# Where the third w_out block and the last modulation stand in a macaron block with pooling and RWKV-7

## The chip, the cores and the metric

One core of a Trainium2 chip runs the whole program once. The metric is the device time of one execution in microseconds (us). TensorE (PE) multiplies matrices, VectorE (DVE) and ScalarE (ACT) work element by element, and SyncE (SP) issues nearly all loads from HBM in one queue. The engines run side by side, each through its own list of instructions in a fixed order; an instruction that waits for another engine or a load holds up all that stand behind it in its list.

## What is computed

One sequence of 256 tokens of width 2048 goes through three sublayers: a gated feed-forward network (FFN), a mixer, and a second FFN. Each sublayer is wrapped in two norms and in a modulation by shift, scale and gate, nine vectors of 2048 that come from one matrix product of the condition `c` with `w_ada` (2048 x 18432, float32).

```python
mod = (silu(c) @ w_ada + b_ada).reshape(B, 3, 3, 2048)      # sublayer, (shift, scale, gate)

def sandwich_sublayer(x, fn, gain_pre, gain_post, shift, scale, gate, weight):
    h = rms_norm(x, gain_pre) * (1 + scale) + shift
    y = rms_norm(fn(h), gain_post)
    return x + weight * (1 + gate) * y

def hybrid_mixer(h, ...):
    p = h @ w_in
    y_pool = multiscale_pool(p[..., :512], ...)
    y_rwkv = rwkv7_time_mix(p[..., 512:], ...)               # 24 heads of 64
    return concatenate([y_pool, y_rwkv], -1) @ w_out         # 2048 x 2048

x = sandwich_sublayer(x, ffn1, ..., mod[0], weight=0.5)
x = sandwich_sublayer(x, hybrid_mixer, ..., mod[1], weight=1.0)
x = sandwich_sublayer(x, ffn2, ..., mod[2], weight=0.5)
```

The FFN is `(silu(h @ w_gate) * (h @ w_up)) @ w_down` with an inner width of 5632. All weights are float32.

## The kernel before

**Matmuls.** Float32 products are made of three matmuls: both operands are split into a rounded part (`hi`) and a rest (`lo`), and hi x hi, lo x hi and hi x lo are summed in PSUM. Weights come in raw tiles of up to 1 MB (`load`, line 174), and `split` (line 180) makes `hi` with a cast on ScalarE (line 186) and `lo` with a subtraction on VectorE (line 187). The activations are held split as `hT` (16 feature tiles of 128, for 256 tokens). All matmuls go through `mul` (line 201), so that most of them have line 202 in the profile.

**Who sets the order.** The program is written in the order of the functions below, but the lists of the engines are made by a scheduler at build time: it goes through the program with estimated durations and gives each engine, whenever it is free, the instruction that is ready and stands first in the program. A later instruction can so move ahead if an earlier one isn't ready. A tile waits for a free slot of its pool. Within the mixer's heads the list of TensorE is fixed by hand (`ordered`), as written. `split` is put 300 instructions ahead in the mixer.

**Modulation.** `ada_begin` (line 222) cuts the nine vectors into columns and the columns into four positions along the 2048 rows. Pre-norm shift and scale of the second FFN, `(7, 6)`, are cut in five, one for each k-block of that FFN (of 2, 2, 4, 4 and 4 feature tiles, `FIRST_BLOCKS`); gates are cut in two. A part of a position of the 4-tile blocks is 512 KB of `w_ada`, in two loads of 256 KB for `(7, 6)` and one of 512 KB for a gate, and one operation on VectorE (line 258) that multiplies it by a value of silu(c) and adds it to an accumulator. Four parts are a position, 16 parts a piece; behind a piece of `(7, 6)`, 16 matmuls with a column of ones (`ada_mod`, line 312) sum over the partitions, and VectorE adds the bias. `ada_step` (line 260) emits one position: load, sum, load, sum and so on. `ada_run` (line 274) is a generator for the mixer that emits one load, and the sum of three loads ago, at each call; it uses `x` (put off to HBM for the while) as its slots and does the modulation up to the third k-block of `(7, 6)`.

**The mixer's end.** The heads are worked off in six groups of two feature tiles (`rwkv_a`, `rwkv_b`), in stages of 12 slots (`stage`, line 883), with matmuls of weights between them as filling (`pieces`). In the last two stages the filling is `last_weights` (line 924): the pooling columns of `w_in`, then the first two of the four 512-column blocks of `w_out` (`out_piece`, line 912, one feature tile for both token halves at a time, six matmuls). The features come in the order 4 to 11, 0 to 3, 12, 13, and at last 14 and 15, which are the last group's heads (`late(14, 15)`). Of the 48 pieces 42 are taken in the two stages. Behind `late(14, 15)` come the other six, then the post-norm operations of these two blocks (`post_rows`), then blocks 2 and 3 with `rows_block` (line 597). Block 2 emits one `ada_step` with each of its four loads: the fourth k-block of `(7, 6)`. Raw tiles of the mixer have two slots, split tiles four.

**The second FFN's begin.** `outer` (line 632) goes over the five k-blocks. For each it makes the block's `hT` (`next_block`, with lines 423 to 428) and goes through ten weight loads, with a `tick` after each. Two of the ten are accumulated in PSUM over all k-blocks; the other eight are spilled to SBUF, and for these the first two k-blocks are merged: in the first k-block they only tick, and load nothing. There are four raw slots of 1 MB and four `ada` slots of 512 KB. Ticks 1, 3, 5 and 7 of the third k-block each emit one `ada_step` (the fifth k-block of `(7, 6)`); the last gate, `(8,)`, takes one step at every twelfth load of the row-wise phase that follows, where the scheduler may move it ahead.

Of the kernel before, what the change touches and what calls it, by code (L numbers as in the profile page):

```python
# [17 lines left out]
P = 128  # L18
# [11 lines left out]
TICKS2 = (1, 3, 5, 7)  # L30
GROUPS = (20, 16, 8)
ADA_AHEAD = ((7, 6), 2)
ADA_FFN1, ADA_FFN2 = 2.8, 12
# [49 lines left out]
class Block:  # L83
# [176 lines left out]
    def ada_step(self, psum):  # L260
        if self.ada_pos == len(self.ada_tasks):
            return
        cols, k0 = self.ada_tasks[self.ada_pos]
        width = cols[0][2]
        per = 512 // width
        if k0 == 0:
            self.acc = self.tile(self.accs, [P, 2, width], tag="acc")
        for kk in range(k0, k0 + 4, per):
            self.ada_sum(self.ada_load(cols, kk, per), self.acc, kk, per)
        self.ada_pos += 1  # L270
        if k0 == KD - 4:
            self.ada_mod(cols, self.acc, self.ada_sums(cols, self.acc), self.tile(psum, [P, 512], tag="mm"))

    def ada_run(self, upto, places):

        todo = []
        for cols, k0 in self.ada_tasks[self.ada_pos:self.ada_end[upto]]:
            per = 512 // cols[0][2]
            todo += [(cols, kk, per) for kk in range(k0, k0 + 4, per)]
        ready = []  # L280
        for n in range(len(todo) + len(places) - 1):
            if len(ready) == len(places) - 1 or n >= len(todo):
                cols, kk, per, raw = ready.pop(0)
                if kk == 0:
                    self.acc = self.tile(self.raws, [P, 4 * T], tag="ada", bufs=self.ada_bufs)[:, :2 * cols[0][2]]
                    self.acc = self.acc.rearrange("p (j c) -> p j c", j=2)
                self.ada_sum(raw, self.acc, kk, per)
            if n < len(todo):
                ready.append((*todo[n], self.ada_load(*todo[n], places[n % len(places)])))
            yield False  # L290
            if n >= len(places) - 1 and kk + per == KD:
                sums = self.ada_sums(cols, self.acc)
                yield True
                self.ada_mod(cols, self.acc, sums, self.bank(self.mod_bank))
                yield False
        self.ada_pos = self.ada_end[upto]
# [374 lines left out]
    def ffn(self, wg, wu, wd, every, mm, actp, blocks, block, outer_tick, first, spill, spare, groups, post_begin, post_done, ahead):  # L671
# [140 lines left out]
    def mixer(self, ctx):  # L812
# [67 lines left out]
        ada = self.ada_run(ADA_AHEAD, [flat_x[:, i * 4 * T:(i + 1) * 4 * T] for i in range(4)])  # L880
# [30 lines left out]

        def out_piece(q, kc):
# [62 lines left out]
        for q in range(2):  # L975
            for tt in range(2):
                self.post_rows(q, tt, 0, 512, banks[q][tt])
        for q, tags in ((2, ("pb", "zb")), (3, ("sb", "y", "mm"))):
            banks = [row(t) for t in tags]

            def load(kc):
                raw = self.load(I["w_out"], 4 * kc, 4, q * 512, 512)
                if q == 2:
                    self.ada_step(self.mm)
                return raw

            def done(tt, c0, n, ps):
                self.post_rows(q, tt, c0, n, ps)

            place = lambda tags: lambda shape: [self.tile(self.w2p, shape, F32R, tag=t) for t in tags]  # L990
            more = [place(t) for t in (("r", "k"), ("v", "bv")) * 2]
            self.rows_block(load, KD, 1, lambda k: self.hT[:, k], banks, q == 3, done, more, self.mm)
# [402 lines left out]
    def run(self):  # L1395
        I = self.I
        self.constants()
        with ExitStack() as ph:
# [15 lines left out]
            self.ffn(I["ffn1_w_gate"], I["ffn1_w_up"], I["ffn1_w_down"], ADA_FFN1, mm, actp, FIRST_BLOCKS, block, tick,  # L1414
# [5 lines left out]
        with ExitStack() as ph:  # L1420
            mm, actp = self.ffn_pools(ph)

            def block(k0, n):
                self.ada_finish(((7, 6), [b[0] for b in FIRST_BLOCKS].index(k0)), mm)
                self.next_block(2, k0, n, mm)

            def tick(q, i):
                if q == 2 and i in TICKS2:
                    self.ada_step(mm)

            self.ffn(I["ffn2_w_gate"], I["ffn2_w_up"], I["ffn2_w_down"], ADA_FFN2, mm, actp, FIRST_BLOCKS,
                     block, tick, FF_OUTER, FF_SPILL, (FF_SPILL + FF_OUTER) // 2 - 8, GROUPS,
                     lambda *a: (self.ada_finish((8,), mm), self.post_begin(2, 0.5, False, mm, *a)),
# [28 lines left out]
```

## Time and profile before

| | |
|---|---|
| median of 3 runs | 2132.65 us (2131.58 to 2134.56) |
| the profiled execution | 2132.83 us |
| its span, first to last instruction | 2131.0 us |
| granted TensorE clock, mean | 0.987 |
| bytes read from HBM | 499.87 MB, 237 GB/s over the span |

A row of the windows view has a stretch of time, the busy time and number of instructions of each engine in it, the granted clock of TensorE (1.00 is full), the busy share of the 16 DMA engines, and GB/s. A row of the order of time has start, duration, engine, line, operation, the tile written and the tiles read, their shape, how often, and in brackets the idle time of the engine before it and who ended it. `PEld` is the loading of the stationary operand, which overlaps the matmuls.

These stages matter here (us from the span's start): the last group's heads until about 1281, the rest of `w_out` until 1359, five padding matmuls and the norms until 1366, and the second FFN's k-blocks from there until about 1612.

### The profile page before, as it was taken

Reading aid. Unit: us, or ns where it says so; the run is one execution under the profiler, and the core shown is the slowest. Engines: PE = TensorE matmul, PEld = TensorE weight load, DVE = VectorE, ACT = ScalarE, POOL = GpSimd, SP = SyncE. Lnnn points to the kernel's source line nnn. Section 1 sums busy time; section 2 is a strip of 40 time slices with the busy share of each in tenths; the row PEclk is TensorE's granted clock in tenths of the full one; section 3 lists DMA queues with packets and bytes.
Section 4 is the critical chain, followed back from the end, with each engine's and each line's share of the span. In section 5 each row is a group of like instructions: output and inputs, shape, how many; then the busy total and the mean of one; then the engine's idle time right before and its main releaser. Section 6 shows DMA issues by size and latency. Waiting matters only on the chain.

```text
span 2131.0 us, 38906 instructions
## 1 busy us (share of the span) xinstructions
PE 2051.9 (96%) x16083; PEld 1829.5 (86%) x16083; DVE 1591.6 (75%) x2204; ACT 1010.5 (47%) x1483; POOL 0.2 (0%) x4
## 2 busy tenths in 40 slices
PE   3999999999999999999999997899999999999998
PEld 3999988888888888898999875789998888888887
DVE  6788898788887876688788968667996555555556
ACT  3544543444434455665555544453454344443453
POOL 0000000000000000000000000000000000000000
PEclk8999999999999999999999999899999999999999
DMA  8989888898989746565555567497875556555563
GB/s 303 352 315 315 291 284 323 308 331 311 320 320 321 267 145 195 174 192 157 147 166 158 167 217 266 158 324 246 317 280 197 190 187 196 181 194 191 187 195 121
DMA packets 315759, 506.62 MB, mean 238 GB/s; under 512 B 13013, under 2 KB 173886, under 8 KB 315070
## 3 DMA queue, kind: packets, MB, share of 16 engines
q1 hardware_dynamic: 314092, 500.78, 69.9%
q10 hardware_dynamic: 1490, 3.36, 0.5%
q8 instruction: 126, 2.06, 0.4%
q14 instruction: 51, 0.42, 0.1%
HBM read 499.87 MB, written 4.22 MB: 237 GB/s over the span
## 4 chain that ended last, share of the span: by engine, by line
PE 81%; DVE 4%; DMA 4%; ACT 1%; issue 1%; SPq 0%; DVEq 0%; ACTq 0%
PE mm L202 47%; PE mm L213 16%; PE mm L214 8%; PE ga L202 2%; PE sb L202 2%; PE sa L202 2%; DMA ada<-in_w_ada_dram 2%; DVE lo L187 1%; PE zb L202 1%; PE pb L202 1%; DMA raw<-in_w_out_dram 1%; PE y L202 1%; DVE acc L258 1%; DMA raw<-in_w_in_dram 1%; ACT hi L186 1%
## 5 line engine op out<-in xcount | busy, mean ns | idle before, releaser
L186 ACT CAST hi<-raw 128x1024 fp32r<-128x1024 f32 (+2 forms) x766 | 695.0, 913 | 873.7 <-PE mm L202 562.3
L187 DVE TENSOR_TENSOR lo<-raw,hi 128x1024 fp32r<-128x1024 f32 (+2 forms) x766 | 799.2, 1051 | 398.8 <-ACT hi L186 396.3
L202 PE MATMUL mm<-hT,hi 128*128 128x256 f32 x3648 | 671.0, 286 | 11.9 <-DVE hT L428 7.2
L202 PEld LDWEIGHTS mm<-hT,hi 128*128 128x128 f32 x3648 | 565.1, 190 | 27.5 <-DVE hT L428 9.0
L213 PE MATMUL mm<-hT,hi 128*128 128x512 f32 x1536 | 539.9, 395 | 0.0
L202 PE MATMUL mm<-hT,lo 128*128 128x256 f32 x1824 | 511.3, 281 | 0.8 <-DVE lo L187 0.7
L214 PE MATMUL mm<-hT,lo 128*128 128x256 f32 x1536 | 431.7, 281 | 0.1
L202 PE MATMUL mm<-hi,act 128*128 128x512 f32 (+1 forms) x1312 | 398.5, 384 | 0.0
L213 PEld LDWEIGHTS mm<-hT,hi 128*128 128x128 f32 x1536 | 288.8, 188 | 67.9
L202 PEld LDWEIGHTS mm<-hT,lo 128*128 128x128 f32 x1824 | 345.4, 190 | 1.5 <-DVE lo L187 1.5
L258 DVE SCALAR_TENSOR_TENSOR acc<-ada,csilu,acc 128x1024 f32<-128x1024 f32 (+1 forms) x247 | 300.5, 1216 | 59.1 <-DMA ada<-in_w_ada_dram 56.8
L214 PEld LDWEIGHTS mm<-hT,lo 128*128 128x128 f32 x1536 | 288.0, 187 | 0.6 <-DVE lo L187 0.5
L202 PEld LDWEIGHTS mm<-hi,act 128*128 128x128 f32 x1312 | 244.3, 188 | 48.6
L202 PE MATMUL mm<-lo,act 128*128 128x512 f32 (+1 forms) x656 | 251.8, 384 | 0.0
L202 PEld LDWEIGHTS mm<-lo,act 128*128 128x128 f32 x656 | 123.3, 188 | 24.4
L669 DVE TENSOR_TENSOR act<-act,mm 128x512 f32<-128x512 f32 x96 | 64.3, 681 | 2.0 <-PE mm L202 1.6
L202 PE MATMUL mm<-ones,acc 128*128 128x1 f32 x96 | 14.7, 281 | 33.3 <-DVE acc L258 33.3
L202 PEld LDWEIGHTS mm<-ones,acc 128*128 128x128 f32 x96 | 14.5, 237 | 34.0 <-DVE acc L258 34.0
L258 DVE SCALAR_TENSOR_TENSOR ada<-x,csilu,ada 128x512 f32<-128x512 f32 (+1 forms) x45 | 41.3, 918 | 0.1
L202 PE MATMUL mm<-hi,work 128*128 128x512 f32 x128 | 40.7, 389 | 0.0
L202 PE MATMUL mm<-hi,hT 128*128 128x512 f32 (+1 forms) x88 | 30.5, 407 | 6.7 <-ACT hT L906 6.7
L423 ACT ACTIVATE hT<-mm,mod,gs 128x256 fp32r<-128x256 f32 x48 | 27.1, 570 | 12.6 <-PE mm L202 12.6
(377 smaller groups left out, 1674.3 us busy)
## 6 DMA issues: line engine op xcount, KB each, us to landing
raw<-in_ffn_w_down_dram SPq DMA_DIRECT2D x88, 1024.0 KB
raw<-in_ffn_w_gate_dram SPq DMA_DIRECT2D x86, 1024.0 KB
raw<-in_ffn_w_up_dram SPq DMA_DIRECT2D x86, 1024.0 KB
ada<-in_w_ada_dram SPq DMA_DIRECT2D x152, 512.0 KB
ada<-in_w_ada_dram SPq DMA_DIRECT2D x192, 256.0 KB
raw<-in_w_in_dram SPq DMA_DIRECT2D x34, 1024.0 KB
x<-in_w_ada_dram SPq DMA_DIRECT2D x64, 256.0 KB
raw<-in_w_out_dram SPq DMA_DIRECT2D x16, 1024.0 KB
```

Source lines behind the costliest of these rows:

```text
L186: a = nc.scalar.copy(hi, raw)
L187: d = nc.vector.tensor_tensor(lo, raw, hi.bitcast(F32), ALU.subtract)
L202: return self.pe(self.nc.tensor.matmul(ps, a, b, start=start, stop=stop))
L213: nc.tensor.matmul(ps.rearrange("p a t -> p (a t)"), hi, x.rearrange("p a t -> p (a t)"), start=start, stop=False)
L214: nc.tensor.matmul(ps[:, 0, :], lo, x[:, 0, :], start=False, stop=stop)
L258: self.later(nc.vector.scalar_tensor_tensor(acc, raw[:, i], ck, acc, ALU.mult, ALU.add))
L423: a = nc.scalar.activation(self.hT[:, k, 0, :], ps[:, j, :], AF.Identity, scale=g, bias=sh)
L669: nc.vector.tensor_tensor(part, part, bank, ALU.add)
```

## The change

Four things are changed.

- Block 2 of `w_out` joins blocks 0 and 1 in `out_piece` and `last_weights`. The program now has: tiles 12 and 13 of blocks 0 and 1 and the splits of their tiles 14 and 15, which are kept in four free tiles of the mixer; then block 2's tiles 4 to 11, 0 to 3, 12 and 13; then tiles 14 and 15 of blocks 0, 1 and 2. The post operations of the three blocks follow, then block 3.
- No modulation is emitted beside `w_out`.
- The second FFN gets its modulation from `ada_run`, which now takes the place of a load as a function, the lag between load and sum (3), the bank, and the place of the accumulator. It covers the fourth and fifth k-block of `(7, 6)` and the gate: 16 + 16 + 32 parts.
- A part is emitted at each of the ten ticks of the first four k-blocks, and then at every third load of the row-wise phase. Before k-block 3 or 4 whatever is missing for it is emitted.

```diff
-TICKS2 = (1, 3, 5, 7)
-ADA_FFN1, ADA_FFN2 = 2.8, 12
+ADA_FFN1, ADA_FFN2 = 2.8, 3
...
-            self.acc = self.tile(self.accs, [P, 2, width], tag="acc")
+            self.acc = self.tile(self.accs, [P, 4 * T], tag="acc")[:, :2 * width].rearrange("p (j c) -> p j c", j=2)
...
-    def ada_run(self, upto, places):
+    def ada_run(self, upto, place, lag, bank, acc_place=None):
...
-        for n in range(len(todo) + len(places) - 1):
-            if len(ready) == len(places) - 1 or n >= len(todo):
-                cols, kk, per, raw = ready.pop(0)
+        for n in range(len(todo) + lag):
+            done = None
+            if n >= lag:
+                done = cols, kk, per, raw = ready.pop(0)
                 if kk == 0:
-                    self.acc = self.tile(self.raws, [P, 4 * T], tag="ada", bufs=self.ada_bufs)[:, :2 * cols[0][2]]
-                    self.acc = self.acc.rearrange("p (j c) -> p j c", j=2)
+                    self.acc = (acc_place() if acc_place else self.tile(self.accs, [P, 4 * T], tag="acc"))
+                    self.acc = self.acc[:, :2 * cols[0][2]].rearrange("p (j c) -> p j c", j=2)
                 self.ada_sum(raw, self.acc, kk, per)
             if n < len(todo):
-                ready.append((*todo[n], self.ada_load(*todo[n], places[n % len(places)])))
+                ready.append((*todo[n], self.ada_load(*todo[n], place(n))))
             yield False
-            if n >= len(places) - 1 and kk + per == KD:
-                sums = self.ada_sums(cols, self.acc)
-                yield True
-                self.ada_mod(cols, self.acc, sums, self.bank(self.mod_bank))
-                yield False
-        self.ada_pos = self.ada_end[upto]
+            if done and (kk + per) % 4 == 0:
+                if kk + per == KD:
+                    sums = self.ada_sums(cols, self.acc)
+                    yield True
+                    self.ada_mod(cols, self.acc, sums, bank())
+                self.ada_pos += 1
+                if kk + per == KD:
+                    yield False
...
+        place = lambda tags: lambda shape: [self.tile(self.w2p, shape, F32R, tag=t) for t in tags]
+        keep = [wide_place("SV"), wide_place("ar"), place("rk"), place(("v", "T1"))]
+
         def out_piece(q, kc):
 
             if q not in banks:
-                banks[q] = [row(t) for t in (("mm", "mm"), ("sa", "ga"))[q]]
+                banks[q] = [row(t) for t in (("mm", "mm"), ("sa", "ga"), ("pb", "zb"))[q]]
             raw = self.load(I["w_out"], 4 * kc, 4, q * 512, 512)
+            parts = []
             for pc in range(4):
                 k = 4 * kc + pc
-                hi, lo = self.split(raw[:, pc:pc + 1, :])
-                for tt in range(2):
-                    self.rows_mm(banks[q][tt], tt, hi[:, 0], lo[:, 0], self.hT[:, k], k == 4, k == KD - 1)
-                yield
+                parts.append((k, *self.split(raw[:, pc:pc + 1, :], keep.pop(0) if keep and k >= 14 else None)))
+                if k == 14:
+                    continue
+                if k == 15:
+                    yield
+                for k, hi, lo in parts:
+                    for tt in range(2):
+                        self.rows_mm(banks[q][tt], tt, hi[:, 0], lo[:, 0], self.hT[:, k], k == 4, k == KD - 1)
+                    yield
+                parts = []
...
-            two = [out_piece(q, 3) for q in range(2)]
-            for q in (0, 0, 1, 1, 0, 0, 1, 1):
-                yield next(two[q])
+
+            ends = [out_piece(q, 3) for q in range(3)]
+            for q in (0, 0, 0, 1, 1, 1):
+                next(ends[q])
+                yield
+            for kc in (1, 2, 0):
+                yield from out_piece(2, kc)
+            for q in (2, 2, 2, 0, 0, 1, 1, 2, 2):
+                next(ends[q])
+                yield
...
-        for q in range(2):
+        for q in range(3):
             for tt in range(2):
                 self.post_rows(q, tt, 0, 512, banks[q][tt])
-        for q, tags in ((2, ("pb", "zb")), (3, ("sb", "y", "mm"))):
...
-                if q == 2:
-                    self.ada_step(self.mm)
...
+        self.rows_block(lambda kc: self.load(I["w_out"], 4 * kc, 4, 3 * 512, 512), KD, 1, lambda k: self.hT[:, k],
+                        [row(t) for t in ("sb", "y", "mm")], True, lambda *a: self.post_rows(3, *a),
+                        [place(t) for t in (("r", "k"), ("v", "bv")) * 2], self.mm)
...
+            bank = lambda: self.tile(mm, [P, 512], tag="mm")
+            ada = self.ada_run((8,), lambda n: self.tile(self.raws, [P, 4 * T], tag="ada", bufs=self.ada_bufs), 3, bank)
 
             def block(k0, n):
-                self.ada_finish(((7, 6), [b[0] for b in FIRST_BLOCKS].index(k0)), mm)
+                while self.ada_pos < self.ada_end[(7, 6), [b[0] for b in FIRST_BLOCKS].index(k0)]:
+                    next(ada)
                 self.next_block(2, k0, n, mm)
 
             def tick(q, i):
-                if q == 2 and i in TICKS2:
-                    self.ada_step(mm)
+                if q < 4:
+                    next(ada, None)
...
-                     lambda *a: (self.ada_finish((8,), mm), self.post_begin(2, 0.5, False, mm, *a)),
+                     lambda *a: (list(ada), self.post_begin(2, 0.5, False, mm, *a)),
```

More of the change, by code (lines that the diff above doesn't have):

```diff
@@ L669, in outer, with ffn @@
                             nc.vector.tensor_tensor(part, part, bank, ALU.add)
-    def ffn(self, wg, wu, wd, every, mm, actp, blocks, block, outer_tick, first, spill, spare, groups, post_begin, post_done, ahead):
+    def ffn(self, wg, wu, wd, every, ada, mm, actp, blocks, block, outer_tick, first, spill, spare, groups, post_begin, post_done, ahead):
         nc = self.nc
@@ L682, in tick @@
             if more and int(chunk / every) > int((chunk - 1) / every):
-                self.ada_step(mm)
+                ada()
         def act(gate, up, spare=False):
@@ L879, in mixer @@
         nc.sync.dma_start(dram, flat_x)
-        ada = self.ada_run(ADA_AHEAD, [flat_x[:, i * 4 * T:(i + 1) * 4 * T] for i in range(4)])
+        ada = self.ada_run(ADA_AHEAD, lambda n: flat_x[:, n % 4 * 4 * T:(n % 4 + 1) * 4 * T], 3,
+                           lambda: self.bank(self.mod_bank),
+                           lambda: self.tile(self.raws, [P, 4 * T], tag="ada", bufs=self.ada_bufs))
         ends = None
@@ L1412, in tick @@
                     self.ada_step(mm)
-            self.ffn(I["ffn1_w_gate"], I["ffn1_w_up"], I["ffn1_w_down"], ADA_FFN1, mm, actp, FIRST_BLOCKS, block, tick,
+            self.ffn(I["ffn1_w_gate"], I["ffn1_w_up"], I["ffn1_w_down"], ADA_FFN1, lambda: self.ada_step(mm), mm, actp, FIRST_BLOCKS, block, tick,
                      FF_OUTER, FF_SPILL, (FF_SPILL + FF_OUTER) // 2 - 8, GROUPS,
@@ L1421, in run @@
             mm, actp = self.ffn_pools(ph)
+            bank = lambda: self.tile(mm, [P, 512], tag="mm")
+            ada = self.ada_run((8,), lambda n: self.tile(self.raws, [P, 4 * T], tag="ada", bufs=self.ada_bufs), 3, bank)
             def block(k0, n):
-                self.ada_finish(((7, 6), [b[0] for b in FIRST_BLOCKS].index(k0)), mm)
+                while self.ada_pos < self.ada_end[(7, 6), [b[0] for b in FIRST_BLOCKS].index(k0)]:
+                    next(ada)
                 self.next_block(2, k0, n, mm)
             def tick(q, i):
-                if q == 2 and i in TICKS2:
-                    self.ada_step(mm)
-            self.ffn(I["ffn2_w_gate"], I["ffn2_w_up"], I["ffn2_w_down"], ADA_FFN2, mm, actp, FIRST_BLOCKS,
-                     block, tick, FF_OUTER, FF_SPILL, (FF_SPILL + FF_OUTER) // 2 - 8, GROUPS,
-                     lambda *a: (self.ada_finish((8,), mm), self.post_begin(2, 0.5, False, mm, *a)),
+                if q < 4:
+                    next(ada, None)
+            self.ffn(I["ffn2_w_gate"], I["ffn2_w_up"], I["ffn2_w_down"], ADA_FFN2, lambda: next(ada, None), mm, actp,
+                     FIRST_BLOCKS, block, tick, FF_OUTER, FF_SPILL, (FF_SPILL + FF_OUTER) // 2 - 8, GROUPS,
+                     lambda *a: (list(ada), self.post_begin(2, 0.5, False, mm, *a)),
                      self.store, False)
```

14 lines of the change are left out of this document (5 added, 9 removed).

## The prediction, made before the changed kernel was run

> **What bounds the kernel now.** I read the page's totals first, then the windows view in 25 us stretches, then whom TensorE waits for, then the order of time around each hole.
>
> ```profile
> span 2131.0 us, 38906 instructions
> PE 2051.9 (96%) x16083; PEld 1829.5 (86%) x16083; DVE 1591.6 (75%) x2204; ACT 1010.5 (47%) x1483; POOL 0.2 (0%) x4
> ```
>
> TensorE is the bound: 2051.9 us busy of 2131.0. The change moves matmuls and takes none away, so it can only win holes and slow clock. The windows view (PE, PEld, DVE, ACT, POOL busy; granted clock; DMA share; GB/s) says where they are.
>
> ```profile
> 1275.00:1300.00 25.00, 18.30 (x71) 14.14 (x70) 21.55 (x33) 11.30 (x26) 0.00 (x0) 0.86 0.66 207
> 1300.00:1325.00 25.00, 22.91 (x101) 17.69 (x99) 20.72 (x35) 11.69 (x26) 0.00 (x0) 1.00 0.86 298
> 1325.00:1350.00 25.00, 14.89 (x75) 13.75 (x76) 13.07 (x26) 7.86 (x14) 0.00 (x0) 0.73 0.30 104
> ...
> 1400.00:1425.00 25.00, 25.00 (x214) 25.00 (x213) 18.12 (x16) 13.75 (x17) 0.00 (x0) 1.00 0.96 327
> 1425.00:1450.00 25.00, 19.74 (x151) 19.35 (x150) 17.12 (x18) 9.98 (x15) 0.00 (x0) 0.86 0.81 278
> ```
>
> The first three are the w_out stage, the last is the second FFN; the 1400 row beside it is full, so TensorE can be kept busy in such work. Its waits from 1240 to 1620 name the causes (total, times, longest):
>
> ```profile
> PE mm L202 <- DVE acc L258: 11.2, 1, 11.2
> PE mm L202 <- ACT hT L906: 6.7, 1, 6.7
> PE mm L202 <- DVE hT L428: 6.0, 4, 5.1
> ```
>
> In order of time on TensorE (start, duration, idle time before it in brackets):
>
> ```profile
> 1266.05 2.05 PE L202 MATMUL sb<-ones,ada 128*128 128x1 f32 x16 [0.39 <-DVE S L1305]
> ...
> 1288.01 0.79 PE L202 MATMUL mm<-hi,hT 128*128 128x512 f32 x1 [6.70 <-ACT hT L906]
> ...
> 1295.36 0.40 PE L202 MATMUL pb<-hi,hT 128*128 128x512 f32 x1
> ...
> 1317.52 0.39 PE L202 MATMUL zb<-hi,hT 128*128 128x512 f32 x1
> ...
> 1335.11 3.58 PE L202 MATMUL mm<-ones,acc 128*128 128x1 f32 x16 [11.17 <-DVE acc L258]
> 1338.54 0.56 PE L202 MATMUL mm<-hi,hT 128*128 128x256 f32 x1
> ...
> 1358.79 4.45 PE L220 MATMUL mm<-consts 128*128 128x512 f32 x10
> ```
>
> From the hole's begin (1288.01 - 6.70 = 1281.3) to the padding matmuls at 1358.8 are 77.5 us. The need: the 96 matmuls of the third column block start from 1295.36 to 1317.52, 0.233 us each, 22.4 us. The fourth block is as much work (half of its rows are 256 wide, in twice the number), and feature tiles 14 and 15 of the first two blocks are 24 matmuls, 5.6 us. With the 16 ones-matmuls at the 2.05 us of the 1266 row the need is 52.5 us, and **25.0 us** are lost: 6.7 waiting for tile 14 of hT; 1.75 since the 24 matmuls from 1288.01 to 1295.36 took 7.35 us, not 5.6 (slow clock); 2.0 between 1317.75 and 1323.94 (1335.11 - 11.17), where the fourth block's first four tiles (three matmuls of 512 and three of 256 columns each, 4.2 us) took 6.2; 11.2 at the ones-matmuls, which stand in TensorE's order ahead of the rest of the fourth block and wait for the modulation's last sum; 1.4 in those (3.43 us to the next start), and the last 2.0 of slow clock behind them.
>
> **The w_out stage after.** 14 of the third block's 16 tiles (84 matmuls, 19.6 us) are put ahead of what needs tile 14. That more than fills the hole, if their weights are there. Two raw slots hold w_out, and the third block's first piece went out when one came free:
>
> ```profile
> 1277.34 0.38 SPq L176 DMA_DIRECT2D raw<-in_w_out_dram  x1
> ...
> 1361.90 0.47 SPq L176 DMA_DIRECT2D raw<-in_ffn_w_gate_dram  x1
> ...
> 1367.85 0.37 SPq L176 DMA_DIRECT2D raw<-in_ffn_w_gate_dram  x1
> ```
>
> ```profile
> 1373.29 1.05 ACT L186 CAST hi<-raw 128x1024 fp32r<-128x1024 f32 x1 [0.68 <-DMA raw<-in_ffn_w_gate_dram]
> ```
>
> ```profile
> 1293.75 0.68 DVE L187 TENSOR_TENSOR lo<-raw,hi 128x512 fp32r<-128x512 f32 x1
> ```
>
> The 1 MB load issued at 1367.85 was cast at 1373.29, 5.4 us later. So the piece issued at 1277.34 is there at 1282.8; with half of such a cast (0.5) and a subtraction (0.68) its first matmul starts near 1284.1, a hole of 2.8 us in place of 6.7. Bounds: 0 (kept splits free the slot sooner) and 6.7 (nothing fills). The slow clock behind it I keep at 1.75, since a shorter hole ahead of the second FFN (1.6 us idle in five) has it too:
>
> ```profile
> 1365.00:1370.00 5.00, 3.39 (x15) 3.19 (x16) 3.95 (x8) 4.10 (x8) 0.00 (x0) 0.67 0.84 270
> ```
>
> The Trainium skill, TensorE: Matmul & The Clock Gate, Part 1, has half speed come after an idle window of about 3.4 us; by it the 2.8 us could pass without, and the end would be 1.75 us earlier. The clock of 0.67 in this row speaks against it.
>
> The 2.0 us for late splits stay (bounds 0 and 7: the two slots now feed the third block at full pace). The ones-matmuls and all their waits leave the stage. The post operations of three blocks come in one burst: 12 on VectorE of 0.68 us for 512 columns and the fourth block's 16 subtractions are 19 us, beside 22.4 us of its matmuls, so they are hidden, by 3 us; the modulation's sums no longer lie between. Sum: 50.4 + 2.8 + 1.75 + 2.0 = 57.0 us in place of 77.5: **-20.5**.
>
> **The second FFN's start.** The fourth k-block's modulation, 16 parts (two loads of 256 KB and one sum each), is now done here, with the fifth's 16 as before and the last gate's 32. Each tick of the first four k-blocks emits one part. The first k-block has ten ticks and only two weight loads (the other eight fall to the merged block), so nine parts, 18 loads, are emitted between its up weights and the next block's gate weights. Does SyncE keep that order? The first FFN has the same case:
>
> ```profile
> 17.71 0.57 SPq L176 DMA_DIRECT2D raw<-in_ffn_w_up_dram  x1
> 18.38 20.29 SPq L248 DMA_DIRECT2D ada<-in_w_ada_dram  x16
> 38.71 0.47 SPq L176 DMA_DIRECT2D raw<-in_ffn_w_gate_dram  x1
> ```
>
> It does: 16 loads went ahead of the next gate weights, though two of four raw slots were free. In the second FFN nothing stands between now (gate weights again at 1361.90, above), and the chain has:
>
> ```profile
> 1360.97 3.91 DMA raw<-in_ffn_w_gate_dram
> ...
> 1376.38 33.26 PE mm L202 x280
> ```
>
> The first 0.52 MB took 3.91 us, 1.6 of it at 327 GB/s, so 2.3 are fixed. After, the 6.8 MB up to and with the second gate weights take 20.8 us more: landed at 1384.1 in today's times, and used 1.8 us later (cast 1.05, half of the subtraction), at 1385.9. Now TensorE is in full work from 1376.4 on, so 9.5 are lost, and 1.75 of slow clock: **+11.3**. Bounds: 0 if only the four parts that find free slots go ahead (3.7 MB, 11.2 us, used at 1376.3); +16.2 at the first FFN's pace (20.3 us for 16 loads, 22.9 for 18, then 3.91 and 1.8). I take the order of the first FFN, the nearest row, with the bandwidth of the second. The Trainium skill, DMA: Bandwidth & Descriptors, Queues, rings and completion order, has each engine consume a ring's descriptors in order, which speaks against this change: the weights stand behind all those bytes. If transfers shared the bandwidth evenly instead, the cost would be near 0; the 3.91 us of the first load, with more issued within 1 us of it, speaks for order.
>
> The ones-matmuls cost their 2.05 us here: **+2.05**. Later weights are covered: one load and one part per 5.7 us of matmuls (48 of 33.26 / 280) are 1.57 MB, 276 GB/s, below the 327 that the 1400 row carried with TensorE full; at 230 GB/s, without that cover, each load would cost 1.1 us.
>
> **The hole at 1430.**
>
> ```profile
> 1432.69 1.28 DVE L258 SCALAR_TENSOR_TENSOR acc<-ada,csilu,acc 128x1024 f32<-128x1024 f32 x1 [2.32 <-DMA ada<-in_w_ada_dram]
> 1433.89 1.09 DVE L428 TENSOR_TENSOR hT<-work,hT 128x256 fp32r<-128x256 f32 x3
> ```
>
> ```profile
> 1434.36 0.58 PE L202 MATMUL mm<-hT,hi 128*128 128x256 f32 x1 [5.07 <-DVE hT L428]
> ```
>
> The next k-block's hT stood on VectorE behind a sum that waited for its load. Of the four such waits the other three are 0.9 together. With loads begun three ahead of their sums I take this one for an ordinary 0.3: 4.8 and 1.75 of slow clock, **-6.5**. Bounds: 0 (the queue is as full as before) and +13 (two more boundaries like it).
>
> **Sum.** 2132.83 (the profiled execution; its span 2131.0 and 1.8 around it; the median of the runs is 2132.65, the same within 0.01%) - 20.5 + 11.3 + 2.05 - 6.5 = **2119.2 us**.
>
> **The rivals.**
> - *The nine parts don't all go ahead.* If a part that waits for a slot lets the second gate weights pass, the start costs nothing: 2107.9 us. For it: two raw slots are free. Against: the first FFN's order.
> - *The hole at 1430 stays, or the start goes at the first FFN's pace.* 2125.7 or 2124.1 us, 2130.6 with both.
> - *Slower: VectorE stands behind sums at every block boundary.* Its queue is in order, and 64 parts instead of 48 now keep the DMA queue full through k-blocks 1 to 4. A boundary costs the 5.07 + 1.75 = 6.8 us of the one seen, 6.5 above an ordinary one. There are three (tiles 4, 8, 12): 2119.2 + 3 x 6.5 = 2138.7 us. It decides once all three stand; with two the time is 2132.2. Against: now two of these boundaries are among the small waits, with the last gate's loads in flight.
> - *The stage isn't filled*: the third block's matmuls stay behind tile 14 for want of weights (two slots), 6.7 instead of 2.8 and 5 more for splits (7 instead of 2): 2128.1 us.
>
> **How the numbers follow.** Forecast (2113 to 2125) 0.50; parts don't all go ahead 0.17; hole stays or slower pace 0.16; stage not filled 0.07; boundaries 0.10. A measurement of this kernel tells about 0.2% (4.3 us) from no change, so faster is below 2128.4 and slower above 2136.9. Faster: 0.50 + 0.17 + 0.10 of the 0.16 = 0.77; slower 0.08 of the 0.10; the rest, 0.15, the same. The range 2107 to 2132 takes in all but the boundaries and the edges of the others, some 0.15.
>
> **What would show it.** Right: third-block matmuls begin near 1284; no ones-matmuls before the padding matmuls, which come near 1338; some 20 part loads between the second FFN's first up weights and its next gate weights, and TensorE idle about ten us there. Wrong: a wait for the hT of tile 14 as long as before, second gate weights issued next to the first, or waits of TensorE for hT L428 beyond 7 us in all.

## The result, and the profile after

| | before | after |
|---|---|---|
| median of 4 runs each | 2132.11 us (2129.74 to 2134.56) | 2116.54 us (2115.35 to 2117.75) |
| ratio | | 0.9927, 95% interval 0.991 to 0.9944 |
| profiled execution | 2132.83 us | 2117.75 us |
| its span | 2131.0 us | 2115.5 us |

The changed kernel is 0.73% faster (0.56 to 0.90). 2119.2 was predicted, 2107 to 2132 as the range. The page's totals of after:

```profile
span 2115.5 us, 38899 instructions
PE 2046.3 (97%) x16083; PEld 1825.0 (86%) x16083; DVE 1592.4 (75%) x2204; ACT 1010.6 (48%) x1483; POOL 0.2 (0%) x4
```

The same number of matmuls, as predicted, and 15.5 us less span. The windows view of after, in the stretches in which the prediction read the losses of before:

```profile
1275.00:1300.00 25.00, 25.00 (x141) 19.97 (x138) 14.06 (x25) 11.89 (x20) 0.00 (x0) 0.99 0.40 135
1300.00:1325.00 25.00, 25.00 (x132) 21.25 (x132) 18.29 (x43) 16.03 (x38) 0.00 (x0) 1.00 0.46 158
1325.00:1350.00 25.00, 22.89 (x129) 18.50 (x128) 17.02 (x49) 11.46 (x33) 0.00 (x0) 0.93 0.42 147
1350.00:1375.00 25.00, 12.57 (x78) 11.90 (x78) 22.78 (x25) 6.81 (x9) 0.00 (x0) 0.66 0.96 335
```

The first two rows, in the w_out stage (which lasts until 1336), are full, at clock 0.99 and 1.00 and with the DMA engines at 40 and 46%. The third has the second FFN's begin in it, and the last, the second FFN's start, is half empty at clock 0.66. TensorE in order of time says the same (start, duration, what, idle time before it):

```profile
1284.67 0.39 PE L201 MATMUL ga<-hi,hT 128*128 128x512 f32 x1
1284.90 0.40 PE L201 MATMUL pb<-hi,hT 128*128 128x512 f32 x1
...
1335.65 4.45 PE L219 MATMUL mm<-consts 128*128 128x512 f32 x10
...
1364.48 1.22 PE L201 MATMUL mm<-hT,hi 128*128 128x256 f32 x4 [12.11 <-ACT hi L185]
```

Block 1 ends with `ga`, block 2 begins with `pb` 0.23 us later, no ones-matmul stands before the padding, and one wait of 12.11 us is new. What the second gate weights waited for stands in SyncE's issues (x18 are nine parts, 17.09 us from the first issue to the last):

```profile
1339.70 17.09 SPq L247 DMA_DIRECT2D ada<-in_w_ada_dram  x18
1356.84 0.43 SPq L175 DMA_DIRECT2D raw<-in_ffn_w_gate_dram  x1
```

Where the time went, by the same instructions in both traces (durations of stretches, us):

| stretch | before | after | difference |
|---|---|---|---|
| until block 1's tile 13 is done | 1281.3 | 1284.9 | +3.6 |
| from there to the padding matmuls | 77.5 | 50.75 | -26.8 |
| to the transposes of the third k-block | 67.63 | 82.95 | +15.3 |
| to those of the fourth | 67.70 | 60.45 | -7.25 |
| to those of the fifth | 59.12 | 60.73 | +1.6 |
| to the first row-wise matmul | 64.32 | 62.25 | -2.1 |

The +1.6 is the second set of ones-matmuls, which stands in that stretch only after the change (1.84 us at 1526.68); the stretch above it has one set before and after.

### The profile page after: what moved, and what is told of

It is laid out like the page before. It is cut to its first block, busy times and chain, and to the rows that moved or that the text cites. A ratio compares the mean times of both kernels' runs of the same rounds, so it can differ in the third digit from the quotient of the medians.

```text
span 2115.5 us, 38899 instructions
## 1 busy us (share of the span) xinstructions
PE 2046.3 (97%) x16083; PEld 1825.0 (86%) x16083; DVE 1592.4 (75%) x2204; ACT 1010.6 (48%) x1483; POOL 0.2 (0%) x4
## 4 chain that ended last, share of the span: by engine, by line
PE 86%; DVE 2%; ACT 2%; DMA 1%; issue 0%; SPq 0%; DVEq 0%; ACTq 0%
PE mm L201 49%; PE mm L212 17%; PE mm L213 9%; PE sa L201 2%; PE ga L201 2%; PE zb L201 2%; PE pb L201 2%; PE sb L201 2%; PE y L201 1%; DVE lo L186 1%; ACT hi L185 1%; DMA raw<-in_w_in_dram 0%; DMA ada<-in_w_ada_dram 0%; DMA raw<-in_ffn_w_gate_dram 0%; DVE x L590 0%
## 5 line engine op out<-in xcount | busy, mean ns | idle before, releaser
L201 PE MATMUL mm<-hT,hi 128*128 128x256 f32 x3648 | 669.4, 286 | 18.4 <-ACT hi L185 13.5
L669 ACT COPY act<-mm 128x512 f32<-128x512 f32 x32 | 18.8, 587 | 28.8 <-PE mm L201 28.8
```

What stands on the lines that cost most here:

```text
L201: return self.pe(self.nc.tensor.matmul(ps, a, b, start=start, stop=stop))
L669: nc.scalar.copy(part, bank)
```

## The experiments

All ratios are to runs of the kernel before on the same chip, with 95% intervals; one kernel's runs spread over 2 to 13 us, so single traces are compared by stretches.

| version | median, us | ratio to before |
|---|---|---|
| changed kernel | 2116.54 | 0.9927 (0.9910 to 0.9944) |
| move only | 2137.07 | 1.0022 (1.0009 to 1.0034) |
| modulation only | 2118.23 | 0.9939 (0.9922 to 0.9955) |
| kept splits unhurried | 2114.14 | 0.9915 (0.9897 to 0.9933) |
| distance 1 | 2117.50 | 0.9934 (0.9919 to 0.9950) |
| small parts only | 2131.19 | 1.0005 (0.9991 to 1.0018) |
| eight slots | 2114.61 | 0.9930 (0.9914 to 0.9947) |
| parts in a queue of their own | 2112.36 | 0.9911 (0.9895 to 0.9927) |
| four parts ahead | 2109.62 | 0.9899 (0.9884 to 0.9914) |
| spread | 2103.95 | 0.9876 (0.9857 to 0.9894) |
| spread in bursts of five | 2117.49 | 0.9945 (0.9929 to 0.9962) |
| late parts | 2102.63 | 0.9865 (0.9847 to 0.9884) |
| late parts, unhurried | 2099.38 | 0.9860 (0.9841 to 0.9878) |

### Which half of the change brings the w_out stage's gain?

The move alone keeps a position of modulation beside each load of the third block, and the second FFN as before:

```diff
             raw = self.load(I["w_out"], 4 * kc, 4, q * 512, 512)
+            if q == 2:
+                self.ada_step(lambda: self.bank("sb"))
...
-                if q < 4:
-                    next(ada, None)
+                if q == 2 and i in (1, 3, 5, 7):
+                    self.ada_step(mm)
```

> The order of w_out's three blocks as changed, but the modulation as before: a position beside each of the third block's four loads, its ones-matmuls in the stage, and the second FFN's steps as before. Theory A (the move fills the hole at tile 14 and the loss at the ones-matmuls belongs to the modulation): the hole of 6.7 and 1.75 of slow clock are gone, the wait of 11 for the last sum stays, the second FFN takes what it took before with its hole of 5 at the third k-block: 2132 - 8 = 2122 to 2126. Rival B (with 8.4 MB of modulation ahead of it in SyncE's queue the third block has no weights when it is wanted): the hole stays or the wait for the sum grows, 2128 to 2136.

TensorE's waits of that version from 1240 to 1620 (total, times, longest):

```profile
PE sb L201 <- DVE acc L257: 14.2, 1, 14.2
PE mm L201 <- DVE hT L430: 6.4, 3, 5.0
```

The hole at tile 14 is gone, but the wait for the modulation's last sum grew from 11.2 to 14.2, and the one for the hT of the third k-block is there as before: the filling only brought TensorE sooner to what it has to wait for. 2137.07 is 1 us above Rival B's range, by the second of its two ways. The trace alone shows no loss against before (its span is 2129.1, the least of its runs); where the median's 0.2% go isn't settled.

The modulation alone keeps the old order of w_out and takes the modulation away from it:

```diff
         for q, tags in ((2, ("pb", "zb")), (3, ("sb", "y", "mm"))):
...
-                if q == 2:
-                    self.ada_step(self.mm)
```

> The modulation as changed (none beside w_out, parts in the second FFN), but w_out's blocks in the order of before: third and fourth behind tile 14. Theory A: the wait of 11.2 at the ones-matmuls, their 3.4 and the slow clock behind go (some 17), the hole of 6.7 with 1.75 stays, and the second FFN takes 7.6 more, as in the changed kernel: 2132 - 17 + 7.6 = 2121 to 2125; the sum of this version's and the move-only version's gains against before, with nothing shared, would then be the whole change's 15.6 within 3. Rival B (the two parts do the same job, and either alone brings most of the stage's 27 us): 2113 to 2117.

```profile
1280.67 0.58 PE L201 MATMUL ga<-hi,hT 128*128 128x512 f32 x1
1285.56 0.80 PE L201 MATMUL mm<-hi,hT 128*128 128x512 f32 x1 [4.30 <-ACT hT L910]
...
1338.82 4.45 PE L219 MATMUL mm<-consts 128*128 128x512 f32 x10
```

From 1281.26 to the padding are 57.6 us: 19.9 of the stage's 26.8 come from taking the modulation out, and the move gives the other 6.8 (the hole of 4.3 with its slow clock) once it is out. Each of these is one trace, that of the modulation alone of its slowest run (2123.18). In the medians the move's share is smaller and uncertain: 0.9939 against 0.9927, with intervals that overlap. The time lies between the two expectations; "nothing shared" fell, since the move alone loses.

### Why was there no hole at all before the third block?

```diff
-                parts.append((k, *self.split(raw[:, pc:pc + 1, :], keep.pop(0) if keep and k >= 14 else None)))
+                parts.append((k, *self.split(raw[:, pc:pc + 1, :], *((keep.pop(0), 0) if keep and k >= 14 else ()))))
```

(the last argument is how far the split is put ahead: 0, not 300)

> The changed kernel, with the splits of tiles 14 and 15 that are kept not put 300 instructions ahead but at their own place. Theory A (the early splits free the raw slot at 1266, and that is why the third block began without the 2.8 us hole that the prediction kept): the third block's first load is issued later, near 1277, and TensorE waits 2 to 5 us before the third block: 2118 to 2122. Rival B (the early casts only stand in the way of the last heads on ScalarE, and the load is in time anyway): 2114 to 2117, no wait at the third block.

Rival B held: no wait at the third block. SyncE issued the third block's first load at 1264.93:

```profile
1264.93 0.38 SPq L175 DMA_DIRECT2D raw<-in_w_out_dram  x1
```

In the changed kernel it was 1266.05, in the kernel before 1277.34, and in the modulation-only version, which keeps no split tiles, 1277.28. It is the keeping of the split tiles that frees the raw slot, not the hurry.

What the hurry does instead stands in two rows of ScalarE and one of TensorE in the changed kernel, and then in ScalarE's row of the unhurried version:

```profile
1257.22 0.61 ACT L185 CAST SV<-raw 128x512 fp32r<-128x512 f32 x1
...
1258.78 0.47 ACT L1296 COPY Q<-zb 128x384 f32<-128x384 f32 x1
```

```profile
1259.30 0.68 PE L201 MATMUL zb<-bt,Q 64*64 64x64 f32 x16 [0.92 <-ACT Q L1296]
```

```profile
1257.09 0.47 ACT L1296 COPY Q<-zb 128x384 f32<-128x384 f32 x1
```

The last heads' copy to Q stands behind the casts for the kept tiles, and TensorE waits 0.92 us for it. Its next wait, for S on VectorE, is 1.29 us; unhurried it is 0.40. In all nine traced versions with hurried splits the two waits are 0.92 and 1.29; in the other five the first is not there and the second is 0.39 or 0.40, so the hurry costs 1.8 us here. The time does not tell the two versions apart (0.9915 against 0.9927).

### What sets the price of the second FFN's start?

**The burst taken away.** No part in the first k-block, 13 in each of the next three:

```diff
-                if q < 4:
-                    next(ada, None)
+                if 0 < q < 4:
+                    for _ in range(1 + (i % 3 == 1)):
+                        next(ada, None)
```

> No part of the modulation is emitted in the second FFN's first k-block; the next three k-blocks emit one part at each tick and a second one at three of the ten ticks (39 calls, as many as must be done before the fifth k-block). Theory A (the burst of parts ahead of the second gate weights costs the 12.1 us of idle TensorE at 1352 and the slow clock behind it, about 15 in all, and nothing else there is short): the second gate weights are issued right behind the first up weights, TensorE's wait for their cast falls below 1 us, and the time is 2116.5 - 13 to 15, so 2101 to 2104. Rival B (bandwidth is short, and the parts only move the lateness): the wait comes back in the next k-blocks, which now carry 13 parts each beside their 9 to 10 MB of weights, and the time stays at 2112 to 2118.

SyncE's issues, then TensorE's waits from 1335 to 1620:

```profile
1336.61 0.37 SPq L175 DMA_DIRECT2D raw<-in_ffn_w_gate_dram  x1
...
1337.53 0.47 SPq L175 DMA_DIRECT2D raw<-in_ffn_w_gate_dram  x1
```

```profile
PE mm L201 <- DVE hT L430: 3.6, 6, 1.2
PE mm L201 <- ACT hT L425: 2.3, 3, 1.5
```

The second gate weights go out 0.9 us behind the first, the 12.1 us are gone, and 2103.95 is Theory A's upper end. From the padding to the third k-block's transposes are 68.5 us (1334.43 to 1402.93), against 82.95 with the burst and 67.63 before.

**A smaller dose.** Four parts behind the first up weights:

```diff
+                if q < 4 and (q or i > 5):
+                    for _ in range(1 + (q > 0 and i in (3, 6))):
```

> As the spread version, but the first k-block emits four parts, as many as there are slots, behind its gate and up weights. Theory A by its own sum: 1.0 MB of weights, 2.1 MB of parts and 0.5 MB of the second gate weights are 3.7 MB, 11.2 us at 327 GB/s and 2.3 fixed, so they land near 1351.3 and are used at 1353.1, where TensorE runs out of work at 1352.4: a wait of 0 to 1 us, and a time as the spread version's within 2 us, 2101 to 2105. If instead each part ahead costs its share of the 12.1 us (nine parts, 1.3 each), four cost 5.4 and the time is 2107 to 2110.

ScalarE in order of time, where the second gate weights are cast:

```profile
1354.82 0.56 ACT L425 ACTIVATE hT<-mm,mod,gs 128x256 fp32r<-128x256 f32 x1 [6.42 <-PE mm L201]
...
1356.63 2.00 ACT L185 CAST hi<-raw 128x1024 fp32r<-128x1024 f32 x2
```

2109.62 is not Theory A's time but the other one, though not for its reason. ScalarE was idle 6.42 us, then did four operations for the next k-block's hT, and only then the cast, which had stood behind them in its list; TensorE waited 2.95 for it. In the spread version's list, made at build time as this one, that cast comes ahead of them, at 1344.86. The transfer came out as in Theory A's sum: by the trace's semaphore events the weights landed at 1354.12, 13.3 us behind the first load's issue (1340.84; the sum has 13.5), and TensorE ran out of work at 1354.78. With the cast at once (1.05, and half of the subtraction, 0.6) they would have been ready near 1355.8, an estimate, and the wait about 1 us. So four parts were still enough to put those weights late, for the most part by the place in a list and not by the transfer.

**Slots or bytes.** Eight slots for the parts, not four, with the engines' lists at the start unchanged (the second FFN's `ada_bufs` is 8):

> The changed kernel with eight slots for the parts in the second FFN, not four; the lists of the engines at its start stay the same. Theory A (the burst ahead of the second gate weights went at the pace at which VectorE's sums, 1.28 us each among the norm's operations, give slots back, not at the bandwidth): the 6.8 MB up to and with those weights flow at 387 GB/s, 17.5 us and 2.3 fixed, and land at 1357.6 in the changed kernel's times, not at 1363.3: TensorE's wait falls from 12.1 to 6 to 7 us and the time to 2109 to 2112. Rival B (bytes set the pace): a wait of 11 to 12.5 us and 2115 to 2118.

```profile
1338.46 13.80 SPq L247 DMA_DIRECT2D ada<-in_w_ada_dram  x18
1352.60 0.38 SPq L175 DMA_DIRECT2D raw<-in_ffn_w_gate_dram  x1
```

```profile
PE mm L201 <- ACT hi L185: 9.0, 1, 9.0
PE mm L201 <- DVE lo L186: 1.8, 1, 1.8
```

The nine parts' issue takes 13.80 us in place of 17.09 and the wait falls from 12.1 to 9.0, so slots are part of the price: in the changed kernel they come back at the pace of VectorE's sums, which the chain of waits has on its way to the second gate weights:

```profile
1349.71 1.03 DVE acc L257
...
1354.77 1.03 DVE acc L257
...
1356.84 6.46 DMA raw<-in_ffn_w_gate_dram
```

But 1.8 come back at the weights' `lo`, behind a sum on VectorE, and the time is the same within the intervals (0.9930 against 0.9927). The 10.8 in all are neither theory's number: eight slots take a quarter off the one wait (3.1 of 12.1), and the bytes, and for 1.8 a sum on VectorE, keep the rest. A slot for every part was not tried.

**Order or bytes.** The parts issued by GpSimd in a queue of their own (`queue=self.nc.gpsimd` for the second FFN's `ada_load`):

> The changed kernel with the second FFN's parts of the modulation issued by GpSimd, in a queue of its own, at the same points of the program. Theory A (it is the order in SyncE's one queue that costs 15 us at the start): the second gate weights are issued next to the first up weights, near 1340; with parts and weights sharing 327 GB/s evenly the 1.5 MB of the first weights would take about twice their own time, 3.0 MB or 9.2 us and 2.3 fixed, and land before TensorE runs out at 1352.4: a wait of 0 to 1 us and 2101 to 2104. Rival B (the bytes themselves are the price, in whatever queue): the second gate weights land behind most of the 5 MB, and the time is 2111 to 2117.

SyncE's issues, a step of the chain of waits, and the DMA queues from 1330 to 1380 (packets, MB, share of the engines):

```profile
1334.55 0.47 SPq L175 DMA_DIRECT2D raw<-in_ffn_w_gate_dram  x1
...
1340.46 0.37 SPq L175 DMA_DIRECT2D raw<-in_ffn_w_gate_dram  x1
```

```profile
1340.46 15.20 DMA raw<-in_ffn_w_gate_dram
```

```profile
q1 hardware_dynamic: 4193, 8.28, 46.0%
q0 software_dynamic: 2426, 7.97, 43.5%
```

The second gate weights now go out next to the first, as Theory A had it, and the next ones, of 1 MB, pay: 15.20 us from issue to landing, and TensorE waits 9.3 for them. The two queues moved nearly the same number of bytes. 2112.36 is Rival B's range: so early, parts cost their bytes in whatever queue they are. The Trainium skill, DMA: Bandwidth & Descriptors, Queues, rings and completion order, has each DMA engine go round the queues it has work for, packet by packet. That the queues take turns agrees with 8.28 and 7.97 MB; turns of one packet each are not shown by these rows, with 4193 and 2426 packets. What helps is to emit them later, not elsewhere.

### What closed the hole at 1430?

The distance of three, put to one (`3, bank` becomes `1, bank`):

> The changed kernel with a part's load begun one ahead of its sum in the second FFN, not three. Theory A (loads begun three ahead are what closed the hole of 5.1 us at the third k-block's start): the wait for the block's hT behind a sum comes back at one block boundary or more, with slow clock, 5 to 7 us each: 2121 to 2124, or more. Rival B (the hole closed because the sums now stand elsewhere, or have four slots and a fixed pace; the distance does nothing): 2115 to 2118, and waits of TensorE for hT of that line below 1.5 us.

```profile
PE mm L201 <- DVE hT L430: 1.6, 4, 0.7
```

Nothing came back (2117.50): the distance of three is not what closed the hole. The grouping, five parts at a time; with it the places change too, 20 parts in the second and 20 in the third k-block, where the spread version has 13 in each of three:

```diff
+                if 0 < q < 3 and i in (1, 3, 5, 7):
+                    for _ in range(5):
+                        next(ada, None)
```

> As the spread version, but the parts come five at a time at four ticks of the second k-block and four of the third, not one or two at each tick. The move-only version had its wait of 5.0 us for the hT of the third k-block, as before; the version with a distance of one had none. Theory A (it is the parts coming one by one, not the distance of three, that keeps VectorE from standing behind a sum that waits for its load): waits of TensorE for hT or for split weights of 4 us or more come back, with slow clock, at one place or two: 2108 to 2118. Rival B (grouping does nothing; the scheduler puts the sums where their loads are due in any case): 2102 to 2106.

```profile
1348.87 14.82 SPq L247 DMA_DIRECT2D ada<-in_w_ada_dram  x10
1363.78 0.38 SPq L175 DMA_DIRECT2D raw<-in_ffn_w_gate_dram  x1
```

```profile
PE mm L201 <- ACT hi L185: 4.7, 4, 2.1
PE mm L201 <- DVE lo L186: 2.9, 3, 1.8
...
PE mm L201 <- DVE hT L430: 1.8, 4, 0.9
```

2117.49, 0.7% more than spread, so bursts of five, 20 in a k-block, cost; which of the two does was not separated. But the hT isn't what waits. With four slots, a burst of five holds SyncE for 10 to 15 us and the weights stand behind it, as at the start. So the kernel before was given the small parts and nothing else of the change:

```diff
-                if q == 2 and i in TICKS2:
-                    self.ada_step(mm)
+                if 1 < q < 4:
+                    for _ in range(1 + (q == 2 and i % 3 == 1)):
+                        next(ada, None)
```

> The kernel before, w_out and its modulation unchanged, with one thing of the change: the second FFN's parts (the fifth k-block's 16 and the last gate's 32) come one or two at a tick of the third and fourth k-block and at every third load behind, loads three ahead of sums, and not four at a time at four ticks of the third. Theory A (the hole of 5.1 us at the third k-block's start, with its slow clock, comes from the parts' grouping and goes with it, whatever w_out does; the prediction's last term, 6.5): no wait for hT above 1.5 us there, and 2129.6 - 6.5 = 2122 to 2126. Rival B (the hole closed in the changed kernel because fewer sums were open when the k-block began): the wait of about 5 stays, and the time is 2128 to 2132.

```profile
PE mm L201 <- DVE hT L430: 7.1, 4, 6.0
```

VectorE in order of time, in that version and then in the changed kernel:

```profile
1430.65 1.28 DVE L257 SCALAR_TENSOR_TENSOR acc<-ada,csilu,acc 128x1024 f32<-128x1024 f32 x1 [2.40 <-DMA ada<-in_w_ada_dram]
1431.85 1.09 DVE L430 TENSOR_TENSOR hT<-work,hT 128x256 fp32r<-128x256 f32 x3
```

```profile
1419.76 1.22 DVE L186 TENSOR_TENSOR lo<-raw,hi 128x1024 fp32r<-128x1024 f32 x1 [1.60 <-ACT hi L185]
...
1422.41 0.41 DVE L430 TENSOR_TENSOR hT<-work,hT 128x256 fp32r<-128x256 f32 x1
1422.74 0.75 DVE L255 TENSOR_SCALAR acc<-ada,csilu 128x1024 f32<-128x1024 f32 x1
```

Rival B held: a wait of 6.0 us, and no gain. The parts of the third k-block's ticks are begun 40 us ahead of it, from 1381.85 on in that version and from 1384.86 in the kernel before, at nearly the same pace: the scheduler draws them forward whatever they are grouped in, and VectorE gets a sum, whose load is late, ahead of the hT. In the changed kernel the burst had done the fourth k-block's parts early, and VectorE had no sum at all between 1403 and 1422; there was nothing to stand behind. The spread versions, and the one with a distance of one, have sums on both sides of that boundary and wait at most 1.2 there, so a sum before the hT need not cost. In the spread version the last two sums ahead of that hT (from 1402.40) start without idle time, their loads landed; the one above waited 2.40 us for its load. What makes the load late was not tried by itself.

### The best version

The spread, with eight parts in the second k-block and 16 in the third and fourth:

```diff
+                if 0 < q < 4:
+                    for _ in range(i > 1 if q == 1 else 1 + (i % 3 != 0)):
+                        next(ada, None)
```

> As the spread version, with eight parts in the second k-block, the first two ticks empty, and 16 in each of the third and fourth. In the spread version TensorE's waits for a k-block's hT were 3.6 us in six and 2.3 in three, and its bytes flowed at 387 GB/s through the second k-block. Theory A (that stretch is short of bandwidth, and the 13 parts there still cost some 2 to 4 us): 2100 to 2102. Rival B (nothing is short there any more; what remains are waits behind sums, which move to the later boundaries): 2103 to 2107.

2102.63: at the border of the two, and no clear difference from the spread (0.9865 against 0.9876), though the waits for hT fell from 5.9 to 2.8 us.

> The late-parts version together with the kept splits at their own place. Theory A (the 0.9 that the last heads wait for ScalarE's copy and the 0.9 of their next wait, both there only with the hurried splits, are on the path): 1.5 to 2.5 below the late-parts version, 2100 to 2101.5. Rival B (the heads' time varies more from run to run than this): 2101.5 to 2104.

2099.38, a little below Theory A's range, is the lowest of all, 1.4% below the kernel before and 0.7% below the changed one, with intervals that do not overlap. In its trace the wait of 0.92 is gone and the other is 0.39. But against the late parts alone (0.9860 and 0.9865) it is not shown to be better.

## Why the prediction was right, and where not

- **What bounds it**: right. TensorE's work is unchanged and the gain is holes and slow clock.
- **The w_out stage, -20.5**: it gave -26.8. The mechanism held; three terms, 6.55 in all, were mis-sized. The hole was to shrink from 6.7 to 2.8 with 1.75 of slow clock kept, since the third block's first piece was put at its old time of issue, 1277.34. The kept splits free the slot 11 us sooner (1266.05), and the hole is 0, its lower bound, and the slow clock with it. The 2.0 for late splits went too, also to their lower bound. The need was worked out as 50.4; 50.75 are left. The working also had most of the gain in the modulation's leaving, and the modulation-only version shows it: 19.9.
- **The second FFN's start, +11.3**: it gave +15.3. The order was right: SyncE sent 18 part loads ahead of the second gate weights, and the spread version wins 11 to 13 back with that alone (by the ratios and by the medians). The size failed at the choice of pace: the bandwidth of 327 GB/s was taken, and the first FFN's pace was put as the bound of +16.2. Four slots, given back by the sums, held the burst to 17.09 us for 18 loads (14.4 at 327 GB/s); eight slots took 13.80. The four slots were weighed only as a reason for parts not to go ahead at all. Of the 4.0 too little, 2.6 are the wait (12.11, not 9.5); the rest is slow clock, 3.2 where 1.75 was put, the clock being at 0.50 from 1365 to 1370 and at 0.90 to 1375.
- **The ones-matmuls, +2.05**: 1.84 us, as they are without a wait:

```profile
1420.38 1.84 PE L201 MATMUL mm<-ones,acc 128*128 128x1 f32 x16
```

- **The hole at 1430, -6.5**: -7.25, the right size for a wrong reason. "With loads begun three ahead of their sums" is the step that failed: with a distance of one the hole is as closed, and small parts three ahead leave it open in the kernel before. In the changed kernel's trace it closed since no sum stood there: the fourth k-block's parts were done before. The sums of the spread version show that a sum whose load has landed need not open it; why a load is late stays open.
- **Not foreseen**: +3.6 ahead of the w_out stage. Half of it, 1.8, are the two waits that the hurried splits make in the last heads, for which the working had no term; the other half is slow clock (the last section). And 2.1 us less in the fifth k-block: the same matmuls at full clock, without a wait to speak of in either trace, and no run explains it.
- **The rivals**: the parts did all go ahead. The slower pace at the start came in part: 17.09 us for 18 loads, where that rival had 22.9; that the loss is near its +16.2 all the same is due to the slow clock. The terms beside it outweighed it. VectorE behind the sums at each boundary did not come: no wait for hT above 1.5 us. The stage was filled.

So the time was right within 3 us by errors that cancelled, which is luck: 6.3 too little won in the stage, 4.0 too little paid at the start, 3.6 lost in the last heads, and 2.1 won in the fifth k-block.

## What to carry to other kernels

Work moved out of a full stage is paid where it lands: look at what the new place holds in front of, in the issuing queue's order, and do not put it where the first weights are still missing; here 12 us were lost again, beside a gain of 27, by the parts of ten ticks. A wait seen behind an operation doesn't say which property of that operation made it, so change one property at a time (distance, grouping, place) before crediting any. And filling a hole gains nothing while a later wait in the same stage ends at the same time: the move alone gained nothing, and the traces show its 6.8 us only once that wait was gone.

## What the runs showed of the hardware

Of the +3.6 us half came from the clock. TensorE has the same short wait ahead of the ones-matmuls in the changed kernel and in the spread version, whose code is the same there:

```profile
1268.09 3.13 PE L201 MATMUL sb<-ones,ada 128*128 128x1 f32 x16 [1.29 <-DVE S L1320]
```

```profile
1270.05 1.95 PE L201 MATMUL sb<-ones,ada 128*128 128x1 f32 x16 [1.29 <-DVE S L1320]
```

In the first the granted clock then fell, in the second it stayed full; and it fell, for less time, in the kernel before, where that wait is 0.39 (windows view of the kernel before, the changed one and the spread version; the clock is the third number from the end):

```profile
1262.00:1280.00 18.00, 17.61 (x135) 13.80 (x136) 7.02 (x14) 5.18 (x9) 0.00 (x0) 0.91 0.63 225
```

```profile
1262.00:1280.00 18.00, 16.71 (x139) 13.39 (x137) 4.67 (x11) 5.04 (x9) 0.00 (x0) 0.81 0.73 287
```

```profile
1262.00:1280.00 18.00, 16.71 (x170) 12.92 (x164) 7.30 (x16) 5.25 (x9) 0.00 (x0) 1.00 0.78 293
```

18 us at 0.81 are 3.4 us lost, at 0.91 1.6, and at 1.00 none: the changed kernel's trace has 1.8 us more of slow clock than that of the kernel before, and the spread version's, with the same two waits as the changed kernel's, none. Such a loss can't be predicted from one trace, and a trace that has it doesn't show what the change did. The Trainium skill, TensorE: Matmul & The Clock Gate, Part 1, names an idle window of some 3.4 us as the condition for half speed; the waits here are 1.29 and 0.39, so the measurement differs from it. What decides it here no run shows.
